# A square that joins the norm's product on its own, two token parts in the first feed-forward's last sums, and residual loads ahead of the norm

## The chip, the cores and the metric

The kernel runs on one core of a Trainium2 chip. The metric is the device time of one execution in microseconds (us), median of three runs. The engines are TensorE (PE, its weight loads PEld), VectorE (DVE), ScalarE (ACT), GpSimd (POOL), and SyncE (SP), whose queue issues nearly all DMA transfers.

## The reference, cut to what matters

Two layers over 1024 tokens of width 1024. Every sub-layer has a norm before it and one after it, and what comes out of the second is added to the residual:

```python
for l in range(DEPTH):
    y = rms_norm(h, norm_g[l, 0])
    ...                                    # layer 0: gated DeltaNet and selected attention
    ...                                    # layer 1: stick-breaking attention and HGRN2
    h = h + rms_norm(y, norm_g[l, 1])      # y: output projection of the mixer
    y = swiglu(rms_norm(h, norm_g[l, 2]), w_gate[l], w_up[l], w_down[l])
    h = h + rms_norm(y, norm_g[l, 3])

def rms_norm(x, g, eps=1e-6):
    return x * lax.rsqrt(jnp.mean(x * x, axis=-1, keepdims=True) + eps) * g
def swiglu(y, wg, wu, wd):
    return (jax.nn.silu(y @ wg) * (y @ wu)) @ wd      # 1024 -> 2816 -> 1024
```

## The kernel before

The tokens are worked on in two halves of 512 columns; a tile is 128 features by 512 tokens in 32 bits, so the width of 1024 is eight tiles (`KD`). Products run in a split form: every operand is a high part (`whi`, `yhi`, `act`) and a rest (`wlo`, `ylo`, a second `act`), and three of the four partial products are made (`passes`, L252). Weights come in units of 128 x 1024: `wload` loads one in two pieces (`wraw`, L233), ACT makes `whi` (L192), DVE one `wlo` and POOL the other (L196); there are buffers for two units. All dense products therefore run in the order in which the program asks for weights; DeltaNet, attention and scan steps are put between them.

The order on each engine comes from a list scheduler: an instruction's place in the program is its priority, and what is traced in `with self.first()` stands ahead of everything that isn't. Weight loads, the clearing of sums, norms and residuals are traced so. A tile is a name (tag) and one of its buffers; an instruction that needs a new tile waits until a buffer of that name is free. `act` has 16 buffers, `hld` 3, `stage` 2, `sq` 2, `part` 10, and the accumulators `acc` in PSUM 3.

What the steps touch:

- `sumsq` (L298 to L307): ACT squares a tile (`ssq` for the first, `sq` for the others), DVE adds it to `ssq`. `inv_rms` (L309): a product with ones sums `ssq` over the features (L313), ACT makes Ln (L315) and Exp (L316): the norm's factor `rs` or `rd`.
- `residual` (L385): for each of eight `k`, a load of the old `h` into `hld` (L396), DVE scales `part` by gain and factor (L397) and adds `h` (L398), SP stores it (L399). With `late` the next `y` is made at once without its own factor (`y_tile`: `yhi` on ACT L339, `ylo` on DVE L343), and `norms` makes the factor `y.r` later, which is applied behind the product. It is a generator; its first `next` traces all of this.
- `outproj` (L415): eight `cat` tiles are loaded into `hld` (layer 0) or `stage` (layer 1) (L427) and split into two `act` tiles each; four pairs of sums follow, each of two units (`cat` 0 to 3, then 4 to 7), copied into `part` (L438).
- `ffn` (L443): 22 hidden tiles in groups of 4, 4, 4, 4, 2, 4; every hidden tile takes two dense units and ends as two `act` tiles; then the group's down products for all eight output tiles `d`, added into `part` by DVE (L489). With `halves` the last group goes through `down_halves` (L494): the four down units are gone through for tokens 0 to 255 and again for 256 to 511, each with a sum of squares of its own (L509, L510). Before, only the last feed-forward does so, and `last_residual` (L513) takes it up, with `h` loaded ahead into `tail` (L519).

The calls, in order (L1310 on): in layer 0 `outproj`, `after_out` and `ffn` of half 0 run among DeltaNet and attention of half 1; `after_ffn(0, 0)` gives the `y` of `proj_d(0)`, behind which comes `outproj(0, 1)`, which needs DeltaNet and attention of half 1 done. In the middle:

```python
every(self.ffn(0, y[0], f))                # layer 0, half 1
r = self.after_ffn(0, 1, f, y, True)
next(r)
o0, y0 = [], []
g = self.outproj(1, 0, o0, "stage")
next(g), next(g)
```

Of the kernel before, what the change touches and what calls it, by code (L numbers as in the profile page):

```python
# [22 lines left out]
P = 128  # L23
# [88 lines left out]
class Trunk:  # L112
# [196 lines left out]
    def inv_rms(self, acc, tag="rs", bank="acc"):  # L309
        nc = self.nc  # L310
        n = acc.shape[-1]
        ps = self.mx(bank)[:, 0:n]
        nc.tensor.matmul(ps, self.ones, acc, start=True, stop=True)  # L313
        r = self.t(self.hp, [P, HS], tag, bufs=1)[:, 0:n]
        nc.scalar.activation(r, ps, AF.Ln, scale=1.0 / D, bias=self.eps)  # L315
        nc.scalar.activation(r, r, AF.Exp, scale=-0.5)  # L316
        return r
# [67 lines left out]
    def residual(self, l, i, src, dst, parts, acc, nxt, box, late=False):  # L385

        nc = self.nc
        with self.first():
            r = self.inv_rms(acc, "rs", "b")
            acc = None  # L390
            y = Y()
            for k in range(KD):
                p = parts[k]
                rows = slice(k * P, (k + 1) * P)
                h = self.t(self.hp, [P, HS], "hld", bufs=3)
                nc.sync.dma_start(h, src[rows])  # L396
                nc.vector.scalar_tensor_tensor(p, p, self.ng(l, i, k), r, op0=OP.mult, op1=OP.mult)  # L397
                nc.vector.tensor_tensor(out=p, in0=p, in1=h, op=OP.add)  # L398
                nc.sync.dma_start(dst[rows], p)  # L399
                if late:  # L400
                    self.y_tile(y, k, p, self.ng(*nxt, k))
                elif nxt is not None:
                    acc = self.sumsq(acc, k, p)
            if late:
                self.norms(y, parts, nxt[1] == 0)
                box.append(y)
# [90 lines left out]
    def down_halves(self, du, act, nd, parts, box):  # L497

        nc = self.nc
        for c in (slice(0, HS // 2), slice(HS // 2, HS)):  # L500
            acc = None
            for d, p in enumerate(parts):
# [5 lines left out]
                with self.first():  # L508
                    nc.vector.tensor_tensor(out=p[:, c], in0=ps, in1=p[:, c], op=OP.add)  # L509
                    acc = self.sumsq(acc, d, p[:, c])  # L510
            box.append((c, acc))

    def last_residual(self, src, dst, parts, halves):  # L513
        nc = self.nc
        with self.first():
# [4 lines left out]
            for i, (c, acc) in enumerate(halves):  # L520
                r = self.inv_rms(acc, ("rs", "rd")[i], "b")
                for k in range(KD):
                    p, h = parts[k][:, c], hs[k][:, c]
                    nc.vector.scalar_tensor_tensor(p, p, self.ng(1, 3, k), r, op0=OP.mult, op1=OP.mult)  # L524
                    nc.vector.tensor_tensor(out=p, in0=p, in1=h, op=OP.add)  # L525
                    nc.sync.dma_start(dst[k * P:(k + 1) * P, c], p)

    def after_out(self, l, half, parts, box, late=False):
# [759 lines left out]
    def run(self):  # L1288
# [31 lines left out]
        every(self.after_out(0, 0, o, y, True))  # L1320
        every(self.ffn(0, y[0], f))
        every(self.after_ffn(0, 0, f, y, True))
        self.proj_d(0, y[1])
# [149 lines left out]
```

## Time and profile before

| what | us |
|---|---|
| median of three runs (2882.89 to 2889.29) | 2888.78 |
| the profiled execution | 2889.96 |
| its span, first to last instruction | 2888.2 |
| TensorE busy | 2819.6 |
| VectorE busy | 1674.9 |
| ScalarE busy | 1580.7 |
| GpSimd busy | 1117.3 |

Busy times are unions of the instructions' durations. Matmuls overlap, so a busy TensorE says that a product was in flight, not that it ran at its peak. The granted clock is the share of full speed that the chip granted TensorE; it has two levels, 1.2 and 2.4 GHz (0.5 and 1), and its mean over the execution is 0.992. A row of the timeline has the start and the length in us, the engine (with q: its queue), the line of the kernel, the operation, the tiles written and read, the shapes, how many instructions were merged, and in brackets the engine's idle time before the first with what ended it.

### The profile page before, as it was taken

Reading aid. Unit: us, or ns where it says so; the run is one execution under the profiler, and the core shown is the slowest. Engines: PE = TensorE matmul, PEld = TensorE weight load, DVE = VectorE, ACT = ScalarE, POOL = GpSimd, SP = SyncE. Lnnn points to the kernel's source line nnn. Section 1 sums busy time; section 2 is a strip of 40 time slices with the busy share of each in tenths; the row PEclk is TensorE's granted clock in tenths of the full one; section 3 lists DMA queues with packets and bytes.
Section 4 is the critical chain, followed back from the end, with each engine's and each line's share of the span. In section 5 each row is a group of like instructions: output and inputs, shape, how many; then the busy total and the mean of one; then the engine's idle time right before and its main releaser. Section 6 shows DMA issues by size and latency. Waiting matters only on the chain. (4 is left out here: it accounts for less than half of the span.)

```text
span 2888.2 us, 42444 instructions
## 1 busy us (share of the span) xinstructions
PE 2819.6 (98%) x14850; PEld 2352.7 (81%) x14850; DVE 1674.9 (58%) x3037; ACT 1580.7 (55%) x2893; POOL 1117.3 (39%) x916
## 2 busy tenths in 40 slices
PE   8999999999999998999999999999999999999997
PEld 6888898878887876988888888889778778888886
DVE  8757964674756557377655235836665545822235
ACT  5555854667666575264665334536666554543334
POOL 3424332344435342255554323226555532333322
PEclk9999999999999999999999999999999999999999
DMA  6443456344333334445333333644333223543333
GB/s 208 135 125 105 149 164 196 97 138 120 98 120 102 104 120 137 146 151 184 114 112 99 95 95 121 238 159 129 95 99 103 92 86 118 185 144 95 97 97 106
DMA packets 261748, 366.69 MB, mean 127 GB/s; under 512 B 23296, under 2 KB 111392, under 8 KB 261536
## 3 DMA queue, kind: packets, MB, share of 16 engines
q1 hardware_dynamic: 261536, 364.00, 40.0%
q8 instruction: 117, 1.92, 0.3%
q14 instruction: 95, 0.78, 0.1%
HBM read 306.23 MB, written 57.67 MB: 126 GB/s over the span
## 5 line engine op out<-in xcount | busy, mean ns | idle before, releaser
L196 POOL TENSOR_TENSOR wlo<-wraw,whi 128x512 fp32r<-128x512 f32 x422 | 588.8, 1395 | 1292.0 <-PE acc L252 526.7
L192 ACT ACTIVATE whi<-wraw 128x512 fp32r<-128x512 f32 x844 | 522.3, 625 | 480.5 <-PE acc L252 385.2
L196 DVE TENSOR_TENSOR wlo<-wraw,whi 128x512 fp32r<-128x512 f32 x422 | 346.2, 821 | 426.5 <-PE acc L252 334.7
L252 PE MATMUL acc<-yhi,whi 128*128 128x512 f32 x2064 | 582.6, 398 | 8.1 <-ACT whi L192 5.9
L252 PE MATMUL acc<-ylo,whi 128*128 128x512 f32 x2064 | 583.4, 398 | 1.0 <-DVE ylo L343 0.9
L252 PE MATMUL acc<-yhi,wlo 128*128 128x512 f32 x2064 | 537.5, 396 | 0.0
L252 PE MATMUL acc<-act,whi 128*128 128x512 f32 (+1 forms) x1984 | 508.1, 393 | 7.0 <-DVE part L489 1.8
L252 PEld LDWEIGHTS acc<-yhi,whi 128*128 128x128 f32 x2064 | 385.3, 189 | 92.7 <-ACT whi L192 6.4
L252 PEld LDWEIGHTS acc<-ylo,whi 128*128 128x128 f32 x2064 | 387.1, 189 | 88.0 <-issue 6.2
L252 PEld LDWEIGHTS acc<-yhi,wlo 128*128 128x128 f32 x2064 | 383.7, 188 | 86.2 <-issue 9.0
L252 PEld LDWEIGHTS acc<-act,whi 128*128 128x128 f32 x1984 | 365.3, 190 | 95.1 <-issue 7.9
L252 PE MATMUL acc<-act,wlo 128*128 128x512 f32 (+1 forms) x992 | 267.1, 387 | 0.8 <-POOL wlo L196 0.8
L252 PEld LDWEIGHTS acc<-act,wlo 128*128 128x128 f32 x992 | 182.4, 188 | 38.1 <-POOL wlo L196 1.6
L959 ACT ACTIVATE pen<-sc,tk 128x384 bf16<-128x384 f32 (+4 forms) x155 | 155.3, 1002 | 41.8 <-DVE tk L963 38.2
L489 DVE TENSOR_TENSOR part<-acc,part 128x512 f32<-128x512 f32 x152 | 103.5, 685 | 66.7 <-PE acc L252 66.6
L192 ACT ACTIVATE act<-stage 128x512 fp32r<-128x512 f32 x104 | 65.3, 629 | 132.9 <-DVE stage L468 114.1
L196 POOL TENSOR_TENSOR act<-stage,act 128x512 fp32r<-128x512 f32 x88 | 117.6, 1337 | 33.7 <-ACT act L192 30.7
L461 DVE TENSOR_TENSOR stage<-acc,stage 128x512 f32<-128x512 f32 x66 | 45.5, 690 | 109.4 <-ACT stage L219 107.3
L306 DVE TENSOR_TENSOR ssq<-ssq,sq 128x512 f32<-128x512 f32 (+1 forms) x119 | 97.2, 817 | 18.7 <-ACT sq L305 15.8
L960 DVE TENSOR_SCALAR tk<-tk 128x1 uint32<-128x1 f32 x186 | 39.2, 211 | 110.6 <-ACT pen L959 109.8
L252 PE MATMUL acc<-whi,yhi 128*128 128x256 f32 x640 | 98.8, 287 | 1.4 <-DVE stage L561 1.0
L252 PE MATMUL acc<-whi,ylo 128*128 128x256 f32 x640 | 97.2, 285 | 0.0
(461 smaller groups left out, 4009.7 us busy)
## 6 DMA issues: line engine op xcount, KB each, us to landing
wraw<-in_w_units_dram SPq DMA_DIRECT2D x844, 256.0 KB, 2.7
h<-part SPq DMA_DIRECT2D x40, 256.0 KB, 4.0
hld<-h SPq DMA_DIRECT2D x40, 256.0 KB, 4.8
qkvT<-stage SPq DMA_DIRECT2D x24, 256.0 KB, 2.3
kT<-kbT SPq DMA_DIRECT2D x24, 256.0 KB, 3.9
vv<-vb SPq DMA_DIRECT2D x24, 256.0 KB, 2.9
qkv<-qkvT SPq DMA_DIRECT2D x18, 256.0 KB, 3.1
part<-in_x_dram SPq DMA_DIRECT2D x16, 256.0 KB, 5.1
```

Of the source, the lines that this page charges most:

```text
L192: nc.scalar.activation(hi, src, AF.Copy)
L196: e.tensor_tensor(out=lo[:, c], in0=src[:, c], in1=hi[:, c].bitcast(F32), op=OP.subtract)
L252: mm(ps, l, r, start=first and g not in begun, stop=last and end[g] == i)
L306: nc.vector.tensor_tensor(out=acc, in0=acc, in1=sq, op=OP.add)
L461: nc.vector.tensor_tensor(out=s, in0=pg, in1=s, op=OP.mult)
L489: nc.vector.tensor_tensor(out=parts[d], in0=ps, in1=parts[d], op=OP.add)
L959: sc.activation(pen, s, AF.Sign, scale=sg, bias=nb, accum_out=n)
L960: v.tensor_scalar(rej.bitcast(U32), n, th, float(1 << b), op0=OP.is_lt, op1=OP.mult)
```

## The change

`inv_rms` takes one tile or a tuple; of a tuple it makes one product each into the same sum. `down_halves` no longer adds the eighth square to `ssq`: it hands over `ssq` and that square as a pair. `residual` loads all eight `h` tiles into `act`, traced ahead of the norm's product, in place of one at a time into `hld`. The first feed-forward (layer 0, half 0) runs with `halves`, and `residual_halves` takes the place of its `after_ffn`: `h` into `act` ahead, then for each 256 tokens the factor, scaling, adding and the split into `yhi` and `ylo`; with the second part the store; then `norms` as before.

```diff
--- before.py
+++ after.py
@@ -308,9 +308,11 @@
 
     def inv_rms(self, acc, tag="rs", bank="acc"):
         nc = self.nc
-        n = acc.shape[-1]
+        accs = acc if isinstance(acc, tuple) else (acc,)
+        n = accs[0].shape[-1]
         ps = self.mx(bank)[:, 0:n]
-        nc.tensor.matmul(ps, self.ones, acc, start=True, stop=True)
+        for i, a in enumerate(accs):
+            nc.tensor.matmul(ps, self.ones, a, start=i == 0, stop=a is accs[-1])
         r = self.t(self.hp, [P, HS], tag, bufs=1)[:, 0:n]
         nc.scalar.activation(r, ps, AF.Ln, scale=1.0 / D, bias=self.eps)
         nc.scalar.activation(r, r, AF.Exp, scale=-0.5)
@@ -386,14 +388,16 @@
 
         nc = self.nc
         with self.first():
+            hs = []
+            for k in range(KD):
+                hs.append(self.act())
+                nc.sync.dma_start(hs[k], src[k * P:(k + 1) * P])
             r = self.inv_rms(acc, "rs", "b")
             acc = None
             y = Y()
-            for k in range(KD):
+            for k, h in enumerate(hs):
                 p = parts[k]
                 rows = slice(k * P, (k + 1) * P)
-                h = self.t(self.hp, [P, HS], "hld", bufs=3)
-                nc.sync.dma_start(h, src[rows])
                 nc.vector.scalar_tensor_tensor(p, p, self.ng(l, i, k), r, op0=OP.mult, op1=OP.mult)
                 nc.vector.tensor_tensor(out=p, in0=p, in1=h, op=OP.add)
                 nc.sync.dma_start(dst[rows], p)
@@ -507,8 +511,12 @@
                 self.passes([(0, ps, [(w(at(j)), [t[:, c] for t in a]) for j, a in enumerate(act)])], 0)
                 with self.first():
                     nc.vector.tensor_tensor(out=p[:, c], in0=ps, in1=p[:, c], op=OP.add)
-                    acc = self.sumsq(acc, d, p[:, c])
-            box.append((c, acc))
+                    if d < KD - 1:
+                        acc = self.sumsq(acc, d, p[:, c])
+                    else:
+                        sq = self.t(self.hp, [P, HS], "sq")[:, 0:HS // 2]
+                        nc.scalar.activation(sq, p[:, c], AF.Square)
+            box.append((c, (acc, sq)))
 
     def last_residual(self, src, dst, parts, halves):
         nc = self.nc
@@ -524,6 +532,30 @@
                     nc.vector.scalar_tensor_tensor(p, p, self.ng(1, 3, k), r, op0=OP.mult, op1=OP.mult)
                     nc.vector.tensor_tensor(out=p, in0=p, in1=h, op=OP.add)
                     nc.sync.dma_start(dst[k * P:(k + 1) * P, c], p)
+
+    def residual_halves(self, l, i, src, dst, parts, halves, nxt):
+
+        nc = self.nc
+        with self.first():
+            hs, y = [], Y()
+            for k in range(KD):
+                hs.append(self.act())
+                nc.sync.dma_start(hs[k], src[k * P:(k + 1) * P])
+                y.t.append(tuple(self.t(self.yp, [P, HS], f"{n}{k}", F32R) for n in ("yhi", "ylo")))
+            accs = []
+            for j, (c, acc) in enumerate(halves):
+                r = self.inv_rms(acc, ("rs", "rd")[j], "b")
+                for k, (p, h) in enumerate(zip(parts, hs)):
+                    hi, lo = (t[:, c] for t in y.t[k])
+                    g = self.ng(*nxt, k)
+                    nc.vector.scalar_tensor_tensor(p[:, c], p[:, c], self.ng(l, i, k), r, op0=OP.mult, op1=OP.mult)
+                    nc.vector.tensor_tensor(out=p[:, c], in0=p[:, c], in1=h[:, c], op=OP.add)
+                    nc.scalar.activation(hi, p[:, c], AF.Copy, scale=g)
+                    nc.vector.scalar_tensor_tensor(lo, p[:, c], g, hi.bitcast(F32), op0=OP.mult, op1=OP.subtract)
+                    if j:
+                        nc.sync.dma_start(dst[k * P:(k + 1) * P], p)
+            self.norms(y, parts, nxt[1] == 0)
+            return y
 
     def after_out(self, l, half, parts, box, late=False):
         cols = slice(half * HS, (half + 1) * HS)
@@ -1318,8 +1350,8 @@
         self.tm_store(U_VB, y1, self.vb[1])
         self.slow = slow
         every(self.after_out(0, 0, o, y, True))
-        every(self.ffn(0, y[0], f))
-        every(self.after_ffn(0, 0, f, y, True))
+        every(self.ffn(0, y[0], f, True))
+        y.append(self.residual_halves(0, 3, self.h[0][0], self.h[1][0], f[0], f[1:], (1, 0)))
         self.proj_d(0, y[1])
         self.finish()
         m0.close()
```

## Rows read from the trace of the kernel before

**Rows 1.** The page: busy times by engine, and one group of PE.

```profile
PE 2819.6 (98%) x14850; PEld 2352.7 (81%) x14850; DVE 1674.9 (58%) x3037; ACT 1580.7 (55%) x2893; POOL 1117.3 (39%) x916
...
L252 PE MATMUL acc<-yhi,whi 128*128 128x512 f32 x2064 | 582.6, 398 | 8.1 <-ACT whi L192 5.9
```

**Rows 2.** Timeline of PE, 1110 to 1132, end of the first feed-forward.

```profile
1114.19 0.73 PE L252 MATMUL acc<-yhi,whi 128*128 128x512 f32 x2 [2.05 <-ACT yhi L339]
...
1130.38 1.07 PE L252 MATMUL acc<-ylo,whi 128*128 128x512 f32 x4
```

**Rows 3.** Stretches: length; busy us (instructions) per engine; clock; DMA share, GB/s.

```profile
1067.00:1091.00 24.00, 23.60 (x106) 18.25 (x105) 23.89 (x37) 11.27 (x19) 11.44 (x10) 1.00 0.23 65
1091.00:1107.00 16.00, 10.57 (x55) 7.66 (x56) 9.92 (x24) 7.30 (x14) 5.32 (x4) 0.89 0.39 116
1107.00:1131.00 24.00, 20.17 (x99) 15.67 (x97) 23.45 (x44) 14.73 (x26) 0.67 (x1) 0.79 0.62 199
```

**Rows 4.** Timeline of SP's DMA issues, 1212 to 1250.

```profile
1214.82 0.46 SPq L853 DMA_DIRECT2D cat<-sq  x1
...
1236.18 0.32 SPq L427 DMA_DIRECT2D hld<-cat  x1
...
1240.19 0.33 SPq L396 DMA_DIRECT2D hld<-in_x_dram  x1
```

**Rows 5.** Timeline of PE, 1225 to 1250.

```profile
1242.21 2.14 PE L252 MATMUL acc<-act,whi 128*128 128x512 f32 x8 [1.03 <-DVE stage L561]
```

**Rows 6.** Timeline of all engines, 2874 to 2880, the end of the program.

```profile
2874.89 1.47 DVE L306 TENSOR_TENSOR ssq<-ssq,sq 128x256 f32<-128x256 f32 x3
...
2876.41 0.80 PE L313 MATMUL b<-ssq,cc 128*128 128x256 f32 x2 [4.05 <-DVE ssq L306]
```

**Rows 7.** Timeline of PE, 1762 to 1800, second feed-forward's end.

```profile
1784.65 1.98 PE L252 MATMUL acc<-act,whi 128*128 128x512 f32 x8
...
1787.37 1.98 PE L252 MATMUL acc<-act,whi 128*128 128x512 f32 x8
...
1798.25 1.98 PE L252 MATMUL acc<-act,wlo 128*128 128x512 f32 x8
```

**Rows 8.** Timeline of PE, 2856 to 2863, down products of 256 columns.

```profile
2858.69 1.12 PE L252 MATMUL acc<-act,whi 128*128 128x256 f32 x8
...
2860.13 1.12 PE L252 MATMUL acc<-act,whi 128*128 128x256 f32 x8
```

**Rows 9.** Lines L509, L398, L397, L524: durations ns min/median/max, first and last start, forms.

```profile
L509 DVE TENSOR_TENSOR part<-acc,part x16: 409/411/425, 2850.5 to 2874.6; 128x256 f32<-128x256 f32 x16
...
L398 DVE TENSOR_TENSOR part<-part,hld x48: 673/680/1484, 572.1 to 2538.0; 128x512 f32<-128x512 f32 x48
...
L397 DVE SCALAR_TENSOR_TENSOR part<-part,gg,rs x48: 736/745/1780, 565.7 to 2522.7; 128x512 f32<-128x512 f32 x48
...
L524 DVE SCALAR_TENSOR_TENSOR part<-part,gg,rs x8: 472/472/1320, 2866.2 to 2869.8; 128x256 f32<-128x256 f32 x8
```

**Rows 10.** Timeline of DVE, 1762 to 1826.

```profile
1794.94 0.69 DVE L196 TENSOR_TENSOR act<-stage,act 128x512 fp32r<-128x512 f32 x1 [2.02 <-ACT act L192]
...
1797.52 6.42 DVE L397 SCALAR_TENSOR_TENSOR part<-part,gg,rs 128x512 f32<-128x512 f32 x8 [0.18 <-ACT rs L316]
1803.87 1.28 DVE L398 TENSOR_TENSOR part<-part,hld 128x512 f32<-128x512 f32 x2
...
1823.11 2.38 DVE L306 TENSOR_TENSOR ssq<-ssq,sq 128x512 f32<-128x512 f32 x2
```

**Rows 11.** Timeline of SP's DMA issues, 1560 to 1600 and 1755 to 1800.

```profile
1576.11 0.33 SPq L1103 DMA_DIRECT2D cat<-oc  x1
...
1759.92 0.42 SPq L427 DMA_DIRECT2D stage<-cat  x1
```

**Rows 12.** Timeline of ACT, 1762 to 1826.

```profile
1775.44 0.63 ACT L192 ACTIVATE act<-stage 128x512 fp32r<-128x512 f32 x1 [1.46 <-DMA stage<-cat]
...
1786.27 0.61 ACT L192 ACTIVATE act<-stage 128x512 fp32r<-128x512 f32 x1
```

## The prediction

> **What bounds the kernel now.** The page first: TensorE is busy in 98% of the span [rows 1], so time can come back only where PE is seen idle, and goes where a new wait reaches it. So I read PE's idle time by place (the waits and the PE timeline) and not the busy shares. The change touches three kinds of place: the end of the first feed-forward, the other residuals, and the end of the program.
>
> At the end of the first feed-forward the down products fill PE up to 1091 (23.60 of 24 us busy) [rows 3], the first product of the next projection waits for `yhi` until 1114.19, and the last `ylo` of the first unit is used at 1130.38 [rows 2]. In between PE has only DeltaNet and sparse-attention steps. The table by stretches [rows 3] gives 5.4 us without PE work in 1091 to 1107 and 3.8 us in 1107 to 1131, and a granted clock of 0.89 and 0.79: at two levels, full and half, a mean of 0.79 over 24 us is 10 us at half speed, 5 us of lost work, and 0.89 over 16 us another 1.8. So about 16 us are lost here. The same rows say what fills the place: VectorE is busy 23.89 of 24 us before, 9.92 of 16 in the middle, 23.45 of 24 after. **VectorE sets this stretch**, but for the 6 us around the norm.
>
> What is late next: the DeltaNet chain's last store at 1214.82, and behind it the eight loads of its output for the second half's output projection, the last at 1236.18 [rows 4]. The products of that projection, just begun, stop for 1.03 us at 1242.21 [rows 5]; they have little slack, so a gain ahead of them passes only in part.
>
> **Part 1, the last square.** On the path at the very end alone: the product waits 4.05 us, until three adds of squares that begin at 2874.89 and last 1.47 us are done [rows 6]. The change leaves out the last (0.41 us by the width) and adds a second product right behind the first; the pair took 0.80 us, so the added one costs some 0.2 to 0.4 us, of which part runs while the last square is made. I take -0.3 us (bounds -0.6 and +0.2). Elsewhere the add's 0.41 us lies in the sum of part 2.
>
> **Part 2, the down sums of the first feed-forward in two parts.** PE: one `d` of 512 columns took 1784.65 to 1787.37, 2.72 us [rows 7]; one of 256 columns, in the last feed-forward, which already works so, 2858.69 to 2860.13, 1.44 us [rows 8]. 16 x 1.44 - 8 x 2.72 = 1.3 us more, hidden while VectorE sets the pace. Four weight units more are loaded and split: 8 DMAs, 8 ACT and 4 GpSimd splits beside engines that have room in [rows 3] (ACT 11.27, GpSimd 11.44 of 24 us), and 4 x 0.69 = 2.8 us of VectorE.
>
> VectorE: narrow instructions cost more than half of wide ones: 0.411 against 0.68 for an add, 0.472 against 0.745 for a product with a column [rows 9]. Down adds 16 x 0.411 - 8 x 0.68 = +1.1; adds of squares 14 x 0.41 - 7 x 0.68 = +1.0; scaling 16 x 0.472 - 8 x 0.745 = +1.6; residual adds +1.1; `lo` (no narrow one in the trace, taken as the scaling) +1.6; with the weights 9.2 us more. What there is to win is the 6.7 us in which VectorE is idle in 1067 to 1131, since the first part's norm can now be made under the second part's products, and what the attention and DeltaNet work there yields to the residual, which has priority: the 57.3 busy us of [rows 3], less 34 for the down adds, squares, residual and weight splits at the durations above, 23 us. Fully yielding, the last `ylo` comes 6.7 + 23 - 9.2 = 20 us earlier; not yielding, 2.5 us later. I take 5 us earlier, nearer to the second end, since VectorE is full from 1067 on, before the first part's sums exist, so most of those 23 us have run by then.
>
> The next projection then ends 5 us earlier, but the eight loads and splits of [rows 4, 5] don't: the last split can't start before the DeltaNet store, which may itself come later for having yielded. I keep **-3 us** of it (bounds -10, all PE idle and half-clock time gone but for what the loads give back, and +3).
>
> First what [rows 3] show, VectorE full on both sides; then the rule: the Trainium skill, Perfetto Trace Analysis, Optimizing Scalar/DVE Operations, says that breaking up instructions can finish work sooner where these engines aren't saturated, and that grouping helps where they are. By the rule's first half the place would give its -10, by its second +3.
>
> **Part 3, the residual's loads, eight at a time into `act`.** It removes waits: before, `hld` has three buffers, and VectorE's in-order adds stood behind DMAs. But at these places PE has other products: the 2064 products that read `yhi` against `whi` waited 8.1 us in the whole kernel, 5.9 of it for weights [rows 1], and of the other 2.2 us 2.05 stand in [rows 2], in the place above. I take -1 us (bounds -3, for waits passed on through other engines, and +1). The eight issues of 0.4 us stand in SP's queue among weight loads; these run two units, 11 us, ahead, and hide them.
>
> What it adds is a claim on the 16 `act` buffers. Two rows tell how buffers are handed out. The loads of `x` for the second half's output residual need nothing but a buffer, yet are issued only at 1240.19, right after the last `hld<-cat` at 1236.18 [rows 4]. And `cat` of the second layer, first half, was stored at 1576.11, yet its first load came at 1759.92, after the feed-forward's last `stage` tile [rows 11]. So **buffers of one name go in the order of the program**, not to who is ready.
>
> Now the second half's first-layer feed-forward. In the program the residual (late, traced whole at its first `next`) stands ahead of the second layer's output projection for half 0. Before, that projection's first four `cat` tiles (eight `act` buffers) were split while the feed-forward's last group held the other eight: the fourth at 1775.44. The fifth waited for the group's release, until 1786.27 [rows 12]. PE went from the last down products, begun at 1784.65, to the projection at 1787.37 without a gap, and its first two units, 48 products with the norm's product between, ended at about 1800 [rows 7]. After the change the residual's eight `h` tiles take the first eight buffers, so:
> - `cat` 0 to 3 get what 4 to 7 had: splits from 1786.27, the last `lo` 1794.94 to 1795.63 [rows 10, 12]. The first unit, 24 products of 0.226 us, then ends near 1798 and not at 1792.8: 5 us.
> - `cat` 4 to 7 wait for the `h` tiles, which the residual's adds release, two for each `cat`. Scaling x8 runs 1797.52 to 1803.94 and the adds follow, two in 1.28 us, from 1803.87 [rows 10]; with the norm's product no longer queued behind others 2 us earlier: 1802 to 1807. Best case, each split runs at once: `cat` 7 is ready at 1808.5, twelve products (2.7 us) later the second unit is done, 1811 against 1800: 11 us. Worst case, the splits stand behind the residual's own `lo` and squares, which have priority on ACT and VectorE (in before these end at 1825.5 [rows 10]; without DMA waits some 5 us sooner): 1820 + 2.7 against 1800, 23 us.
> - Filling: the third accumulator bank lets 12 products of the next pair go ahead, -2.7 us. No other PE work is at hand: attention and scans of half 1 need the residual's `y`.
> - After such a gap the clock falls, as in [rows 3]: 2 to 5 us.
>
> Sum: 11 - 2.7 = +8 at the low end, 23 - 2.7 + 5 = +25 at the high end; I take **+17**, the middle. What queues behind the waiting splits: on ACT and VectorE the weight splits of the next units, on SP the other `stage` loads, on PE all dense work; and PE has no slack later in which it could be made good.
>
> The Trainium skill has this as a reading rule (Perfetto Trace Analysis, Optimization Strategy): repeated bubbles on an engine that should be full can mean that there isn't enough SBUF to allocate the next tile. The trace agrees: between the fourth and the fifth split lie 10.8 us [rows 12]; by the rule alone no price follows.
>
> **Sum.** -0.3 - 3 - 1 + 17 = +12.7 us on the profiled run's 2889.96 us (1.8 over its span): 2902.7. That run is 1.2 us over the median of three, so 2901.5, **2902 us**.
>
> **Rivals**, on the same base.
> 1. The buffers' queue stays short (low end, +8) and the first feed-forward's end gives its whole -10: -3.3, **2886**, no change to be seen. For it: the splits are short (0.6 us) and ACT has gaps; against: VectorE's full rows.
> 2. The other side: the claim on `act` costs nothing, since buffers go to whichever tile is ready and `cat` comes ahead of `h`. Then -4.3: **2885**. Against it, the two waits of [rows 4, 11]; it decides when `cat` 0 is split before the last down group ends.
> 3. The same, and the first feed-forward's end gives -13, its 16 us but for 3: -0.3 - 13 - 1, **2874**, faster. It needs VectorE to yield fully there as well.
> 4. The change doesn't do what it says: VectorE is full, so the first part's norm is not ready under the second part's products (+3), and the queue is long (+23): **2913**.
>
> **How the numbers follow.** Measurement tells 0.3%, 8.7 us, from no change: faster is below 2880, slower above 2897.5. Forecast (2898 to 2909) 0.45, rival 4 0.15, rival 1 0.15, rival 2 0.15, rival 3 0.10. Faster 0.10, same 0.30, slower 0.60. The range leaves out rival 3 and the worst of rival 4: 2881 to 2917.
>
> **What would show it.** Right: `act<-stage` splits of the second layer's first output projection starting near 1786 (shifted by what came before) and not 1766, in two bunches with the residual's adds between, and PE gaps there of 10 us or more with a fallen clock. `h` loads into `act` at the last group of each feed-forward. Part 2: narrow down adds, the next projection's first product 5 us closer to the last down product, VectorE still full. Part 1: the last `ssq` wait at the end shorter by about 0.3 us. Wrong: no gap after that feed-forward, or a PE gap at the first feed-forward's end that is gone.

## The result and the profile after

The changed kernel takes 2909.99 us, median of four runs (2908.33 to 2912.57), against 2887.34 us for the kernel before in the same runs (2882.89 to 2889.29): 22.7 us more, ratio 1.0076 (95% interval 1.0058 to 1.0095). The forecast was 2902 us, +12.7, in a range of 2881 to 2917. The profiled run took 2912.57 us. From the page, the span, the busy times and the group of PE that answers to the last row of [rows 1]:

```profile
span 2910.7 us, 42798 instructions
...
PE 2827.7 (97%) x14956; PEld 2361.9 (81%) x14956; DVE 1686.3 (58%) x3076; ACT 1592.5 (55%) x2919; POOL 1117.8 (38%) x920
...
L252 PE MATMUL acc<-yhi,whi 128*128 128x512 f32 x2064 | 579.8, 397 | 7.0 <-ACT whi L192 5.6 <-ACT yhi L341 1.0 <-ACT yhi L553 0.2
```

PE has 8 us more of busy time for a span 22.5 us longer. VectorE has 11.4 us more work, of which 9.2 were expected at the end of the first feed-forward.

**Where the time went.** Two traces are laid side by side by the weight splits (`whi<-wraw` on ACT): the same split in both, and how much later it starts than in the trace of before. The kernels e1 to e10 are those of the experiments below; us, worked out from the starts of the splits.

| split, by its time in before | after | e1 | e2 | e3 | e5 | e7 | e9 | e10 |
|---|---|---|---|---|---|---|---|---|
| 172.84 | +6.1 | +4.0 | +4.5 | +5.1 | +4.5 | +4.2 | +1.2 | +0.8 |
| 1065.60, last down group, first feed-forward | +6.4 | +2.9 | +4.6 | +6.8 | +5.7 | +4.8 | +2.8 | -1.1 |
| 1186.01, end of the next projection | +10.9 | +7.7 | +3.0 | +9.6 | +10.2 | +4.3 | +2.1 | -12.1 |
| 1304.17, after the output projection | +10.9 | +7.5 | +2.8 | +9.8 | +9.8 | +5.0 | +1.6 | -8.7 |
| 1602.88, attention and scans done | +5.7 | +2.2 | -2.4 | +5.7 | +6.2 | -2.5 | -4.2 | -13.3 |
| 1767.15, last groups of the second feed-forward | +5.7 | +2.2 | -2.4 | +5.7 | +6.2 | -2.5 | -4.2 | -13.3 |
| 1837.69, next output projection running | +20.7 | +1.5 | +12.2 | +5.1 | +18.5 | -3.1 | -4.7 | -13.8 |
| 2860.81, the program's end | +21.6 | +4.0 | +12.6 | +6.0 | +19.2 | -3.9 | -4.4 | -14.2 |

The first row must be read first. Up to 172.84 all these programs have the same instructions in the same order, and yet the traces differ by up to 6 us: that is the difference of one run from another (the trace of before is a quick one there, and a slow one again between 1304 and 1603, where e2, whose PE order is that of before up to 1686, gains 5). A step between two rows is therefore good to some 3 to 5 us where attention and scans run, and to less than 1 us where only dense products do, as from 1602 on. In after the one large step is from 1767.15 to 1837.69, 15.1 us (15.9 by the last row); the end of the first feed-forward costs 4.4.

**The end of the second feed-forward.** SP's DMA issues, and then the splits of `cat` on ACT:

```profile
1765.59 0.42 SPq L431 DMA_DIRECT2D stage<-cat  x1
...
1772.58 1.85 SPq L394 DMA_DIRECT2D act<-h  x4
1774.53 0.38 SPq L431 DMA_DIRECT2D stage<-cat  x1
1775.00 1.80 SPq L394 DMA_DIRECT2D act<-h  x4
...
1791.89 0.33 SPq L431 DMA_DIRECT2D stage<-cat  x1
```

```profile
1790.50 0.63 ACT L192 ACTIVATE act<-stage 128x512 fp32r<-128x512 f32 x1 [1.77 <-PE acc L252]
...
1797.84 0.63 ACT L192 ACTIVATE act<-stage 128x512 fp32r<-128x512 f32 x1 [1.27 <-DMA stage<-cat]
...
1806.79 0.63 ACT L192 ACTIVATE act<-stage 128x512 fp32r<-128x512 f32 x1 [5.89 <-DVE part L402]
...
1817.66 0.63 ACT L192 ACTIVATE act<-stage 128x512 fp32r<-128x512 f32 x1 [0.45 <-DMA stage<-cat]
```

The eight `h` tiles take the free `act` buffers at 1772 to 1777; no `cat` is split there, as the first four were in [rows 12]. It isn't their loads that the splits wait for: the first two `cat` tiles, issued at 1765.59 and 1774.53, landed 3.4 and 4.0 us later, and the first was split only at 1790.50. The first four splits come in one bunch from 1790.50 to 1797.84, in the buffers of the last down group, and the other four from 1806.79 to 1817.66, after VectorE's adds (L402), which give the `h` tiles back:

```profile
1799.75 6.41 DVE L401 SCALAR_TENSOR_TENSOR part<-part,gg,rs 128x512 f32<-128x512 f32 x8 [0.55 <-ACT rs L318]
...
1806.08 1.28 DVE L402 TENSOR_TENSOR part<-part,act 128x512 f32<-128x512 f32 x2
...
1807.89 3.69 DVE L402 TENSOR_TENSOR part<-part,act 128x512 f32<-128x512 f32 x6
```

What PE does with it (timeline of PE; compare [rows 7], where the last down products went into the projection without a gap and its second unit's last eight products began 11.8 us after the last four of the down group):

```profile
1791.44 1.07 PE L252 MATMUL acc<-act,wlo 128*128 128x512 f32 x4
...
1795.18 1.19 PE L252 MATMUL acc<-act,whi 128*128 128x512 f32 x4 [1.24 <-DVE act L196]
...
1807.48 0.82 PE L252 MATMUL acc<-act,whi 128*128 128x512 f32 x2 [4.57 <-ACT act L192]
...
1814.76 1.21 PE L252 MATMUL acc<-act,whi 128*128 128x512 f32 x2 [1.80 <-DVE act L196]
...
1821.85 1.99 PE L252 MATMUL acc<-act,wlo 128*128 128x512 f32 x8
```

Here they begin 30.4 us after. In the stretches of after (length; busy us and instructions of PE, PEld, DVE, ACT, POOL; clock; DMA share; GB/s), first three as [rows 3], shifted by 6 us, and then this place:

```profile
1073.00:1097.00 24.00, 21.22 (x148) 19.57 (x149) 23.75 (x38) 12.39 (x25) 13.95 (x10) 0.93 0.56 182
1097.00:1113.00 16.00, 13.19 (x98) 11.76 (x97) 15.96 (x33) 9.80 (x22) 8.97 (x8) 1.00 0.38 119
1113.00:1137.00 24.00, 16.98 (x90) 12.66 (x90) 21.47 (x65) 13.35 (x29) 0.67 (x1) 0.86 0.50 164
1793.00:1807.00 14.00, 8.30 (x32) 5.53 (x31) 11.27 (x16) 4.80 (x9) 2.77 (x2) 1.00 0.44 131
1807.00:1823.00 16.00, 12.04 (x30) 7.66 (x31) 15.48 (x25) 11.89 (x21) 0.00 (x0) 0.68 0.53 181
```

The last row has the fallen clock: 0.68 over 16 us is 10.2 us at half speed, up to 5.1 us of lost work. With the 9.7 us in which PE has no work in the last two rows that makes at most 14.8 us, near the 15.1 of the table.

**The end of the first feed-forward.** The three stretches show that the idle time of PE did not go; it moved. Before it stood in the middle (10.57 of 16), where VectorE was idle too. Now VectorE is busy there (15.96 of 16), and PE is idle in the last one (16.98 of 24). The timeline of PE says on what (below it, VectorE's first scaling of the residual):

```profile
1104.06 0.60 PE L315 MATMUL b<-ssq,cc 128*128 128x256 f32 x2
...
1107.76 0.63 PE L252 MATMUL acc<-act,wlo 128*128 128x256 f32 x4
...
1115.02 1.05 PE L809 MATMUL a<-tn,nt 128*128 128x128 f32 x8
1122.06 2.08 PE L814 MATMUL a<-tt,y 128*128 128x128 f32 x8 [5.99 <-DVE y L810]
...
1131.56 1.84 PE L252 MATMUL acc<-yhi,whi 128*128 128x512 f32 x6
```

```profile
1108.54 2.45 DVE L551 SCALAR_TENSOR_TENSOR part<-part,gg,rs 128x256 f32<-128x256 f32 x6
```

The first part's down products were done by 1090, but VectorE came to its adds so late that its norm's product ran at 1104.06 and its scaling at 1108.54, behind the last down products of the second part (1107.76). So hardly anything of the first part's residual ran under the second part's products. A DeltaNet step then waits 6 us for VectorE, which has the first part's residual adds and `ylo` steps, squares of the second part and attention steps to do. The next projection starts at 1131.56, 62.4 us after the group's first down product; in before 51.5 us. From the last down product it is 23.4 us, in before 23.7: not 5 us closer, as the prediction's sign had it.

**The end of the program.** The two products that follow the last adds of squares (timeline of all engines; compare [rows 6]):

```profile
2897.24 1.47 DVE L306 TENSOR_TENSOR ssq<-ssq,sq 128x256 f32<-128x256 f32 x3
...
2898.77 0.70 PE L315 MATMUL b<-ssq,cc 128*128 128x256 f32 x2 [1.91 <-DVE ssq L306]
2899.31 0.59 PE L315 MATMUL b<-sq,cc 128*128 128x256 f32 x2
```

### The profile page after: what moved, and what is told of

It is laid out like the page before. It is cut to its first block, busy times and chain, and to the rows that moved or that the text cites. A ratio compares the mean times of both kernels' runs of the same rounds, so it can differ in the third digit from the quotient of the medians.

```text
span 2910.7 us, 42798 instructions
## 1 busy us (share of the span) xinstructions
PE 2827.7 (97%) x14956; PEld 2361.9 (81%) x14956; DVE 1686.3 (58%) x3076; ACT 1592.5 (55%) x2919; POOL 1117.8 (38%) x920
## 5 line engine op out<-in xcount | busy, mean ns | idle before, releaser
L192 ACT ACTIVATE whi<-wraw 128x512 fp32r<-128x512 f32 x852 | 528.6, 626 | 513.3 <-PE acc L252 415.4
L252 PE MATMUL acc<-act,whi 128*128 128x512 f32 (+1 forms) x2048 | 516.4, 389 | 24.3 <-ACT act L192 5.9
L252 PEld LDWEIGHTS acc<-act,whi 128*128 128x128 f32 x2048 | 372.2, 192 | 113.8 <-issue 11.7
```

Source lines behind the costliest of these rows:

```text
L192: nc.scalar.activation(hi, src, AF.Copy)
L252: mm(ps, l, r, start=first and g not in begun, stop=last and end[g] == i)
```

## The experiments

Two theories for the large step. **A, the claim**: the residual's `h` tiles stand ahead of `cat` in the order in which `act` buffers are given out. **B**: the residual's place and priority, whatever its buffers. For the end of the first feed-forward: **A, VectorE is full** and the parts add work to it; **B, order**, the residual's steps go ahead of those that PE could live on. Where an edit says `ahead`, that many of the eight `h` tiles are loaded into `act` ahead, and the others through `hld` as before. `y_first`, `gp` and `cut` are arguments that are set for the first feed-forward alone. The diffs show the lines that matter.

**e1: the change without the claim.**

```diff
+        ahead = 0 if (l, i) == (0, 3) else KD
```

> The changed kernel, but the residual behind the second feed-forward (layer 0, half 1) takes its eight h tiles from hld as before; all else as changed. Theory A, that these tiles take the place of cat in act: cat 0 to 3 are split before the last down group ends, PE has no gap between the last down product and the output projection, and the 15.9 us that the changed kernel loses between the weight splits at 1767 and 1837 (offset +5.7 to +21.6) go: the offset stays within 2 us there, and the time is 2894 us, give or take 3. Rival B, that the stall comes from the residual's priority or from its place in the program and not from the buffers: the 16 us stay, 2910.

Measured 2894.34 us, ratio 1.0023 (1.0014 to 1.0033). The offset goes from +2.2 to +1.5 over the place. ACT, and PE from the last group into the projection:

```profile
1772.73 1.24 ACT L192 ACTIVATE act<-stage 128x512 fp32r<-128x512 f32 x2 [2.75 <-DMA stage<-cat]
1776.68 0.63 ACT L192 ACTIVATE act<-stage 128x512 fp32r<-128x512 f32 x1 [1.33 <-DMA stage<-cat]
1787.65 0.62 ACT L192 ACTIVATE act<-stage 128x512 fp32r<-128x512 f32 x1
```

```profile
1789.00:1803.00 14.00, 14.00 (x62) 11.21 (x61) 11.42 (x16) 8.18 (x14) 3.71 (x3) 1.00 0.40 121
1803.00:1819.00 16.00, 16.00 (x72) 13.25 (x71) 15.63 (x21) 11.01 (x20) 3.71 (x3) 1.00 0.75 257
```

The `cat` splits are ahead of the group's end again, and PE is busy in 30 of 30 us at full clock, where after had 20.3 of 30.

**e2: the claim alone, in the kernel before.**

```diff
+        ahead = KD if (l, i, nxt) == (0, 3, (1, 0)) and dst is self.h[1][1] else 0
```

> The kernel before with one thing of the change: the residual behind the second feed-forward loads its eight h tiles into act ahead of the norm. Theory A: the whole loss of that place comes back, +16 us (13 to 19), ratio 1.0055, with cat splits in two bunches and a clock below 0.8 between them. Rival B, that the loss needs the shifted schedule of the other parts: under +5 us.

Measured 2903.56 us, ratio 1.0054 (1.0039 to 1.0069): 15.4 us more than before, and an offset from -2.4 to +12.2 over the place. The splits come in the same two bunches, and the clock falls:

```profile
1789.72 0.63 ACT L192 ACTIVATE act<-stage 128x512 fp32r<-128x512 f32 x1 [1.18 <-DMA stage<-cat]
1798.67 0.63 ACT L192 ACTIVATE act<-stage 128x512 fp32r<-128x512 f32 x1 [5.89 <-DVE part L408]
```

```profile
1785.00:1799.00 14.00, 8.27 (x32) 5.48 (x31) 11.34 (x16) 4.87 (x9) 2.76 (x2) 0.99 0.43 130
1799.00:1815.00 16.00, 11.77 (x32) 7.97 (x33) 15.46 (x26) 12.15 (x22) 0.00 (x0) 0.69 0.53 181
```

The loss comes with this one edit and goes with it. Theory B for the place falls: in e1 the residual has the same place and priority. (A kernel that loads the eight tiles ahead into buffers of their own was not run. The two `cat` tiles that had landed and were not split speak against the early loads themselves as the cause.)

**e5: half the claim**, in the changed kernel.

```diff
+        ahead = KD // 2 if (l, i) == (0, 3) else KD
```

> The changed kernel, but the residual behind the second feed-forward loads only its first four h tiles into act ahead; the other four come through hld as before. Theory A, buffers of one name go in the order of the program: cat 0 and 1 are split before the last down group ends, cat 2 to 5 get that group's buffers, only cat 6 and 7 wait for h tiles, so of the 15.9 us that eight claimed tiles cost (weight splits at 1767 to 1837) about half is left, 5 to 11 us: 2899 to 2905. Rival B, all or nothing, since the last cat waits for the residual's adds either way: 14 to 16 us, 2908 to 2910. Rival C, nothing is lost while any cat is split in time: 2894.

Measured 2907.94 us, ratio 1.0058 (1.0044 to 1.0071). The step is 12.3 us (+6.2 to +18.5) of the 15.1, between the numbers of A and B; by the ratios it is 10.1 us (against e1's 1.0023) of 15.3, A's upper end. Splits on ACT:

```profile
1780.08 0.63 ACT L192 ACTIVATE act<-stage 128x512 fp32r<-128x512 f32 x1 [1.46 <-DMA stage<-cat]
...
1799.84 0.63 ACT L192 ACTIVATE act<-stage 128x512 fp32r<-128x512 f32 x1 [0.78 <-DMA stage<-cat]
1810.23 0.61 ACT L192 ACTIVATE act<-stage 128x512 fp32r<-128x512 f32 x1
1813.53 0.62 ACT L192 ACTIVATE act<-stage 128x512 fp32r<-128x512 f32 x1
```

Who is split when is as A says: two early (the second at 1780.08), four from the group's release, two after the adds. But the loss is not halved. It fits the time at which the *last* `cat` is split, here 1813.53, less the run's own 6.2 us 1807, against 1812 with eight tiles: VectorE does all eight scalings before the first add, so the first buffer comes back late whether four are claimed or eight.

**e3: the parts alone**, in the kernel before: the first feed-forward in two parts with `residual_halves`, sums of squares complete, the other residuals from `hld`. (`residual_halves` itself loads its eight `h` tiles ahead, so that much of the loads is in it.)

```diff
-        every(self.ffn(0, y[0], f))
-        every(self.after_ffn(0, 0, f, y, True))
+        every(self.ffn(0, y[0], f, True))
+        y.append(self.residual_halves(0, 3, self.h[0][0], self.h[1][0], f[0], f[1:], (1, 0)))
```

> The kernel before with the first feed-forward's end in two parts of the tokens alone (with the sums of squares complete, as before, and the other residuals from hld). Theory A, VectorE is full there, so the two parts only add work: the last down product ends some 11 us later than in the kernel before, proj_d's end 4 us later, and the time is 2887 to 2893 by how much of it is given back before 1600. Rival B, that the two parts pay and the residual's loads spoiled it: the first product of the next projection comes earlier than in the kernel before, 2880 to 2885.

Measured 2895.19 us, ratio 1.0022 (1.0013 to 1.0032): +7.0 us, beyond the 2893 of A's upper edge. The last down product comes 37.7 us after the group's first, not 27.8, and the projection's first product 62.4 and not 51.5 us after it.

**e4: the loads ahead, everywhere but in the claim's place.** No parts, no pair.

```diff
+        ahead = 0 if dst is self.h[1][1] else KD
```

> The kernel before with the loads ahead into act in all residuals but the one behind the second feed-forward; no parts, no pair. Theory A: the 7 us that the changed kernel wins back between 1304 and 1350 come from the loads of the output residual of half 1 in layer 0 and show here, -4 to -7 us: 2881 to 2884. Rival B: they are only the slack that the late end of the first feed-forward left, and show nowhere without the parts: 2886 to 2889. My own term was -1.

Measured 2882.57 us, ratio 0.9984 (0.9975 to 0.9994): -4.6 us by the ratio, between 1.7 and 7.2. The kernel has the loads ahead in six residuals, not only in the change's five: the one behind the first feed-forward is among them, whole, which the change has in parts. The groups of VectorE's adds of `h` (columns: busy us, mean ns, idle before and its releaser) in before, in e2, where all but the claim's still come through `hld`, and in e4:

```profile
L398 DVE TENSOR_TENSOR part<-part,hld 128x512 f32<-128x512 f32 x48 | 35.9, 756 | 13.3 <-DMA hld<-in_x_dram 7.1 <-DMA hld<-h 6.2
```

```profile
L408 DVE TENSOR_TENSOR part<-part,hld 128x512 f32<-128x512 f32 x40 | 33.0, 834 | 7.8 <-DMA hld<-h 4.1 <-DMA hld<-in_x_dram 3.7
```

```profile
L408 DVE TENSOR_TENSOR part<-part,act 128x512 f32<-128x512 f32 x40 | 28.6, 754 | 0.0
```

The waits are gone, as they were meant to. The window 1304 to 1350, on which theory A's size rested, is not a good witness: e2 and e3, which have nothing of the loads there, gain 4 to 5 us in it against the trace of before.

**e7: the loads and the pair.** As e4, with the pair for the last square at the program's end.

```diff
-                    acc = self.sumsq(acc, d, p[:, c])
-            box.append((c, acc))
+                    if d < KD - 1:
+                        acc = self.sumsq(acc, d, p[:, c])
+                    else:
+                        ...
+            box.append((c, (acc, sq)))
```

> The kernel of the loads elsewhere (2882.57 us, -5.6) with the pair for the last square at the program's end besides. My term was -0.3 (bounds -0.6 to +0.2) for the pair. Theory A, from the ends of the runs so far: from the split at 2860.8 to the last instruction the kernels with the pair took 0.7 and 0.95 us more than the kernel before, those without it 0.3 to 0.5 more, so the pair costs about 0.4 us: 2883. Rival: it gives 0.3 us, the tail's length is at or below that of the runs without it.

Measured 2885.80 us, ratio 0.9985 (0.9977 to 0.9994), no different from e4. From the split at 2860.81 to the end, the four kernels with the pair took 0.95, 0.73, 0.46 and -0.06 us more than before (after, e1, e7, e5), and the nine without it -0.1 to 0.6 more. The pair gives nothing and costs nothing that can be seen.

e7 also makes the cleanest comparison for the parts: e1 differs from it in them alone, and stands at 1.0023 against 0.9985, 0.0038 or 11 us.

**e6: the parts' sums of squares on GpSimd.** As e3.

```diff
-                    acc = self.sumsq(acc, d, p[:, c])
+                    acc = self.sumsq(acc, d, p[:, c], nc.gpsimd if y_first else None)
```

> The kernel of the halves alone (2895.19 us, +7.0), with the fourteen narrow adds of squares of the first feed-forward's end on GpSimd in place of VectorE. Theory A, VectorE is full there and its added 9 us are what makes the two parts slower: 14 x 0.41 = 5.7 us less on VectorE bring 3 to 6 us back, 2889 to 2892. Rival B, it is the order (the residual's steps run ahead of DeltaNet's and attention's, which PE then waits for): no more than 1.5 us comes back, 2894 or more.

Measured 2896.32 us, ratio 1.0018 (1.0009 to 1.0027). Nothing of note came back, so by its own numbers B. But the stretch of 64 us from the group's first down product shows that it was no test; e3 first, then e6:

```profile
1069.00:1133.00 64.00, 48.95 (x332) 42.55 (x331) 61.26 (x135) 38.40 (x80) 26.00 (x20) 0.95 0.46 152
```

```profile
1069.00:1133.00 64.00, 45.54 (x306) 39.38 (x305) 57.66 (x123) 36.77 (x79) 41.02 (x34) 0.87 0.49 160
```

GpSimd, 26.00 us busy, is now at 41.02, and the norm's product waits for it:

```profile
1114.50 0.70 PE L315 MATMUL b<-ssq,cc 128*128 128x256 f32 x2 [2.91 <-POOL ssq L306]
```

The wait had been handed on: GpSimd still had 23 of 64 us free, but each add took longer there and stood behind its other work. (By the Trainium skill, Perfetto Trace Analysis, Optimizing Scalar/DVE Operations, moving work between these two might not help, since they share a port. The time agrees; whether the port has a part in it, no run here shows, since a narrow add cost 0.95 us on GpSimd against 0.41 on VectorE and GpSimd had its weight splits to do.)

**e9: the parts with less work.** As e3, the twelve inner squares left out.

```diff
-                    acc = self.sumsq(acc, d, p[:, c])
+                    if d in (0, KD - 1) or not y_first:
+                        acc = self.sumsq(acc, d, p[:, c])
```

> The kernel of the halves alone (2895.19 us), whose first feed-forward's end takes only the first and the last square of each part into the sum; the twelve others (an ACT square and a VectorE add each) are left out, so that its norm is not the reference's. No engine gets the work instead, and the last step ahead of the norm stays. Theory A, VectorE is full there and its added work is what makes the parts slower: 12 x 0.41 = 4.9 us less on VectorE bring 3 to 5 us back by the end of the next projection (weight splits at 1186), 2890 to 2892. Rival B, order: the second part's residual, ahead of DeltaNet's and attention's steps by priority, leaves PE without work whatever VectorE has before it: at most 1.5 us back, 2893.5 or more.

Measured 2888.63 us, ratio 0.9999 (0.9990 to 1.0008): nothing of e3's loss is left, 6.6 us back by the ratio for 4.9 us less on VectorE (and 5.0 less on ACT, which was not full). From 1065 to 1186 it gains 0.7 us where e3 loses 2.8. The same 64 us:

```profile
1065.00:1129.00 64.00, 52.64 (x352) 45.66 (x351) 59.07 (x135) 35.68 (x71) 25.74 (x20) 0.92 0.52 171
```

Theory A, VectorE's work, stands, with more back than the 3 to 5 us that were expected; B as the only cause falls.

**e8 and e10: less work on VectorE without the parts.** As e4; in e8 seven wide adds of squares go to GpSimd, in e10 six squares are left out.

```diff
-                            acc = self.sumsq(acc, d, parts[d])
+                            acc = self.sumsq(acc, d, parts[d], nc.gpsimd if gp else None)      # e8
-                        if f0 + ng == NF:
-                        if f0 + ng == NF:
+                        if f0 + ng == NF and (d in (0, KD - 1) or not cut):                    # e10
```

> The kernel of the loads elsewhere (2882.57 us), with the seven wide adds of squares of the first feed-forward's last sums on GpSimd in place of VectorE, no parts. Theory A, VectorE sets the pace of that place: 7 x 0.68 = 4.8 us less on VectorE, the last one dearer by some 0.6 us on the path to the norm: -2 to -4 us, 2879 to 2881. Rival B, the last sum's way to the norm and the attention steps set it: 2882 to 2884.

> The kernel of the loads elsewhere (2882.57 us), no parts, whose first feed-forward's last sums take only the first and the last of eight squares (six ACT squares and six VectorE adds left out; the norm there is not the reference's). Theory A: 6 x 0.68 = 4.1 us less on VectorE bring the next projection 3 to 4 us forward, seen at the weight splits at 1186. How much of it stays: if the output projection behind it is held by DeltaNet's last store and the loads after it, as the step -3 of the prediction said, less than half, 2881 to 2883; if not, all, 2878 to 2880. Rival B, VectorE's work is not what holds the place: no gain at 1186 either.

e8: 2887.79 us, ratio 0.9989 (0.9980 to 0.9998), no better than e4 and above what either theory expected. e10: 2881.02 us, ratio 0.9974 (0.9962 to 0.9987), 2.9 us better than e4 by the ratios, whose intervals overlap. The 64 us of e7 (which is e4 there) and of e10:

```profile
1067.00:1131.00 64.00, 52.17 (x246) 39.19 (x245) 55.59 (x105) 32.42 (x57) 19.97 (x16) 0.92 0.46 148
```

```profile
1061.00:1125.00 64.00, 56.48 (x285) 43.16 (x284) 54.03 (x108) 36.38 (x63) 20.54 (x17) 1.00 0.47 153
```

For 4.1 us less on VectorE PE wins 4.3 us and the full clock, and from 1065.60 to 1186.01 e10 gains 11.0 us (e7 0.5), where 3 to 4 were expected. By 1304.17, past the output projection, 7.6 are left; by 1602.88, 12.2 against e7's 7.4, that is 4.8, and in the measured times 3. So as far as single traces tell, more than half of what is won at this place is given back. DeltaNet's last store came 154.5 us after the group's first down product, against 155.3 in e7, though the output projection began 164.1 us after it, not 172.8: it ran up against the store and the loads behind it. Worked out in the same way, the trace of e8 has won 5.2 us by 1186.01 and has none of it left at 1304.17; its store came after 160.2 us. So the moved adds may have helped at the place itself, though the time doesn't show it.

**e11 and e12: which residual?** Loads ahead in the output residual of half 1 in layer 0 alone (e11), and in e4's others without it (e12).

```diff
+        ahead = KD if (l, i) == (0, 1) and not late else 0                                     # e11
+        ahead = 0 if dst is self.h[1][1] or ((l, i) == (0, 1) and not late) else KD            # e12
```

> The kernel before with the loads ahead in one residual alone, that behind the output projection of half 1 in layer 0 (x from DRAM). Theory A, the gain of the loads (-5.6 us in five residuals) sits there, where VectorE's adds waited for x behind the loads of cat: -3.5 to -5, 2883 to 2885, weight splits from 1304 to 1350 some 4 us closer than in a kernel without it. Rival B, it is spread over the residuals at about 1 us each: 2887 or more.

> The complement of the run before it: loads ahead into act in the four residuals other than those behind the output projection of half 1 in layer 0 and behind the second feed-forward. The one residual alone gave nothing (2889.54 us, ratio 1.0000, interval 0.9992 to 1.0009), although its profiled run was 7 us short of the profile of before. Theory A, the gain of the loads (ratio 0.9984 and 0.9985 in two kernels) sits in these four, where VectorE's adds waited 4 to 6 us for h and 2 to 4 for x: ratio 0.998 to 0.999, and no VectorE idle time for hld outside the two residuals left. Theory B, neither part gives anything alone, the gain needs all five or is smaller than it seemed: ratio 0.999 to 1.001.

e11: 2889.54 us, ratio 1.0000 (0.9992 to 1.0009). e12: 2887.51 us, ratio 0.9995 (0.9986 to 1.0004). (The others are five, as the loads in e4 are six.) Neither half shows the gain of the whole, which e4 and e7 have at 0.9984 and 0.9985; both came out as theory B had it. But the intervals are as wide as the gain, and e12's overlaps those of e4 and e7, so a gain spread over the residuals isn't excluded. Where it sits stays open.

## Why the prediction was right, and where it was not

**The claim on `act`: right in its place, cause and size.** +17 was forecast (+8 to +25); e2 measures +15.4, e1 to after 0.0053 of the time, +15.3, the traces 15.1 and 15.9. Both bunches, the adds between them and the fallen clock came as described, and 9.7 us of PE gaps where 10 or more were named: first split 1790.50 less the trace's 5.7 us is 1784.8 (forecast 1786.27), the last lo, ended at 1820.49, is 1814.8 (forecast 1808.5 to 1820). The rows that told it were two that had nothing to do with the change, loads that the working read as late for want of a buffer alone [rows 4, 11]. The working had the buffers' release as the thing that decides, and e5 fits it, against its own expectation: half as many tiles cost two thirds (by the ratios) to four fifths (by the traces) of the time. One reading was loose: the 10.8 us that it held up as the trace's agreement lie between splits on ACT, while PE had no gap there [rows 7]; PE's gaps came with the change.

**The parts: the wrong sign.** The step that failed is "I take 5 us earlier" and the "-3 us" made of it (bounds -10 and +3). The parts alone cost 7.0 us (e3), and against the same kernel without them, both with loads ahead, 11 (e1 and e7). The terms of VectorE's work were right: narrow adds and products took 0.41 and 0.47 to 0.48 us, and the 64 us of [rows 3] hold 61.2 us of VectorE work after the change against 57.3. Three things were wrong in the working.

- It took for granted that "the first part's norm can now be made under the second part's products". It wasn't: the first part's scaling began at 1108.54 in after, behind the last down products at 1107.76, and in e3 at 1112.5 behind 1107.2. VectorE, which had attention steps to do besides, was busy for 39.7 of the 40 us from 1073 to 1113.
- The 5 us on the way to `y` came with the loads, not with the parts. The first product with a `wlo`, which follows those of all `yhi` and `ylo` with the unit's `whi`, stood 75.9 us behind the group's first down product in before and 70.7 in e3, but 67.1 with the loads ahead and no parts (e7; e4 66.9), and 72.8 with both (e1; after 72.4). Like for like, the parts made this way 5.7 us longer, where the working had at worst 2.5.
- The same work stands in the way of the DeltaNet and attention steps, which need VectorE too, and which are all that PE has until `y` is there. I wrote that DeltaNet's last store "may itself come later for having yielded", and gave it no price. The store came 152.1 us after the group's first down product in before and 156.5 in after, the output projection's first product at 174.0 and 178.5. Of that, the parts alone account for 1.7 us at the store (155.3 in e7, 157.0 in e1) and 5.2 at the projection (172.8 and 178.0): that is about what the way to `y` is longer, and what the later store adds to it isn't shown apart. e9 shows that it is VectorE's work: 4.9 us less of it, and the loss is gone.

The rule that was weighed there (the Trainium skill, Perfetto Trace Analysis, Optimizing Scalar/DVE Operations: breaking up where there is room, grouping where there is none) pointed the right way by its second half. The trace agrees with that half: VectorE was busy for 61.2 of 64 us, and e3 lost 7.0 us. Rival 4 had the mechanism, "VectorE is full, so the first part's norm is not ready under the second part's products"; its +3 had the right sign and half the size or less.

**What is late next: right, as far as single traces tell.** That the place's gain would pass only in part is what e10 shows: 11 us won at 1186, about 3 at the end, within the noise of the comparison with e4. It would also be why a repair of the place was worth little.

**The loads elsewhere: too small.** -1 us (bounds -3 and +1), measured -4.6 (-1.7 to -7.2) and -4.3 (-1.7 to -6.6) in two kernels with six residuals ahead, not the change's five. The step looked at PE's waits for `yhi` alone and found 2 us. What the waits for `hld` held was VectorE itself, 13.3 us of idle time in before and none in e4 where `h` comes from `act`, at places where others queue for it. That this is the way the gain comes about is argued and not shown, since neither half of the loads shows it alone.

**The last square: no effect**, -0.3 forecast within -0.6 and +0.2. In after three adds still end last [rows 6], now those of the fifth to the seventh square; the eighth square, ready 0.07 us before they end, waits for nothing and saves nothing.

**The sum.** +17 came as 15.4, -1 as -4.6, -3 as +6.4 to +11, -0.3 as nothing. Without the claim the change costs 6.6 us (e1), with it 21.9 by the ratio. The forecast of slower was carried by one term, and its 10 us of error by another. That the total missed by no more was in part luck: the loads' gain, 3 to 4 us larger than forecast in e4 and e7, stood against the parts' loss. The parts (+6.4) and the loads (-4.6) of e3 and e4 would add up to +1.8 where e1 has +6.6; the difference is the loads ahead at the first feed-forward, which e4 counts and the parts already contain, or the width of the intervals; that stays open. Of the kernels that leave nothing out the quickest are e4 and e7, some 0.15% below before: the loads without the parts and without the claim.

## What to carry to other kernels

Before a tile is loaded ahead into a name that others use, look who is next in the program for that name, and price it by when the last of them now gets a buffer, which here depended on when the newcomers were given back more than on how many they were. Splitting work into parts to start the next stage sooner adds work to the engine that does the narrow steps: count it against every chain that needs this engine, also those that merely fill the time. And where a place has a second limit close behind the first, test with less work, not with moved work: e9 and, in its trace, e10 answered what e6 and e8, which moved it to an engine where it takes longer and the norm waits for it, left open.

## What the runs showed of the hardware

Two programs with the same order of instructions were up to 6 us apart within the first 173 us of their traces, and the kernel e11, whose profiled run ended 6.8 us ahead of the profile of before, was no faster in its twelve runs (2883.25, the profiled one and the quickest, to 2894.22). At this length a pair of single traces tells where a step of 15 us is; one of 5 us, where attention and scans run, needs more than one of each.
